# Twenty stores move from the SyncE queue to GpSimd, and sixteen gate loads are issued one product sooner

## The chip, the cores and the metric

The kernel runs on one core of one Trainium2 chip, as one launch. The core has TensorE (PE: matmuls, with a sequencer that loads weights, PEld), VectorE (DVE), ScalarE (ACT), GpSimd (POOL) and SyncE (SP). Each takes its own instructions in order and waits on semaphores for the others. DMA transfers are issued by SP, ACT and POOL and move data between on-chip memory and DRAM. The metric is device time in microseconds, the median of several executions.

## The reference

One decoder layer on x of shape 1 x 1024 x 1024, float32, cut to what matters here:

```python
h = rmsnorm(x, pre_g)
proj = h @ w_in    # [z_ssm | xBC | dt | q | k | v | f | z_att | g_ssm | g_att]
# A: Mamba-2 scan, 16 heads in 4 groups, 8 chunks of 128 positions
yg = ssd(conv_silu(xBC), dt) * silu(z_ssm)
y_ssm = yg * rsqrt(mean(yg*yg over the group) + eps) * ssm_norm_g
# B: forgetting attention, 16 heads, causal, softmax(q.k/8 + F[t] - F[s]) @ v
y_att = o * silu(z_att)
merged = sigmoid(g_ssm) * (y_ssm @ w_branch_ssm) + sigmoid(g_att) * (y_att @ w_branch_att)
out = x + rmsnorm(merged @ w_out, post_g)
```

The pieces that the change touches are y_ssm of the fourth group (the normed recurrence), silu(z_att) (attention's gates) and sigmoid(g_ssm) (the gates of the recurrence branch).

## The kernel before

**Products.** Every large matmul runs as three matmuls on high and low parts of the operands (names ending in h and l). The projection, the two branch products and the output product go through `Pair`: two blocks of 128 output columns times 1024 positions, done as seven products in the order 1, 2, 6, 5, 7, 4, 3 with sums of weights and of activations in place of an eighth. Each product is 12 matmuls of 128x512 into a PSUM bank (`pb`, `pc`, `pd`). Weights come by `raw<-in_wu` (L344, SP's queue, six buffers; a load waits for the last reader of the buffer that it overwrites), are summed on DVE (`sum`, L357 and L373; in place at L381), and split on ACT (L351) and DVE (L352) into `wop`, which has four buffers. `Pair.give` takes a finished product out of PSUM: ACT at L412, DVE at L414, L416 and L418. `keep` (L404) holds a partial one in `s`.

**Stages.** `Stream` is one fixed list of steps (pair, product) run in halves between other work. Until about 690 us that other work is the scan, group by group, with 8 chunks each. On POOL a chunk has `xe` (L872), `ce` (L879) and the state `new` (L893), which TensorE reads in its `yps` matmuls. At the end of a group `gate_and_norm` scales the four half rows `xs` (L1006) and stores them to `ys_dram` (L1010, SP's queue). Then comes attention, eight head pairs in six groups each: scores `s<-k,q`, a mask `far<-beyond` (`beyond` on POOL L1307, cast on DVE L1311), a row minimum on DVE (L1474, `nm`), the exponential on ACT (L1478, `ex`), transposes on TensorE (`pt`), copies `p` (L1515, L1517) and `av<-p,v`. The rest of the products runs between these groups.

**The pairs that matter.** The late pairs `za` (attention's silu gates, four pairs) run at the end of the scan and the start of attention. Their handler `silu_gate` does a tanh on ACT (L636), a multiply on DVE (L637) and the store `za_dram<-th` on SP's queue (L638). The pairs `gs` and `ga` store the tanh of the merge gates to `gs_dram` and `ga_dram` (ACT's queue, L622). From about 970 us the recurrence branch's product runs in four pairs with the handler `gated`: `begin` loads one 128x512 half of a gate (L1053, `th<-gs_dram`, SP's queue) as the step that finishes that half begins, and one half step after the result was taken from PSUM `times` multiplies it (L1062, DVE) and stores it from POOL (L1063, `ms_dram`). All of these 128x512 tiles named `th` come from one ring of four buffers (`small()`). In these pairs activations are fetched into `x0l` and the like on SP (L265) and split on ACT (L280, `x0h`) and DVE (L281). The mask rows `fb` are loaded on SP (L1335) and completed on POOL (L1342).

**What sets the order.** The program is written by a scheduler that places each instruction by its own estimate of when it can run, except for those pinned to program order; TensorE's order is fixed. Each engine then keeps its list. A DMA also waits for the one issued eight places before it in the same kind of queue, since eight semaphores go round for SP and ACT and eight for POOL. The instruction numbers in names (`th_6674`) are buffer numbers of the built program.

Of the kernel before, what the change touches and what calls it, by code (L numbers as in the profile page):

```python
# [23 lines left out]
NG = 4  # L24
# [62 lines left out]
def hybrid_layer(ctx: ExitStack, tc, a, out):  # L87

    nc = tc.nc
# [25 lines left out]
    za_dram = tc.dram_tile([NK, P, T], F32, name="za_dram")  # L115
    gs_dram = tc.dram_tile([NK, P, T], F32, name="gs_dram")
# [6 lines left out]
    ys_dram = tc.dram_tile([NK, P, T], F32, name="ys_dram")  # L123
# [8 lines left out]
    def turn(out_, in_, idn=ident):  # L132
        return tc.keep_in_program_order(nc.tensor.transpose(out_, in_, idn))  # L133

    def pin(op):
        return tc.keep_in_program_order(op)

    def small(name="th"):
        return gp.tile([P, HALF], F32, tag="th", name=name)
# [182 lines left out]
    class Pair:  # L322
# [95 lines left out]
                    nc.vector.tensor_tensor(d, s, ps, ALU.subtract)  # L418
            post(ch)

        def do(self, which):
            if which in (2, 4, 3) or which in (5, 7) and self.sums:
                unit, ch = {2: (0, 0), 4: (1, 0), 3: (0, 1)}.get(which, (1, 1))
                for begin in self.handlers[unit][2:]:
                    begin(ch)
            if which == 1:
                pool, tag = self.bank
                self.b = pool.tile([P, HALF], F32, tag=tag, bufs=1, name="pb")
                yield from self.matmuls(self.b, 1, "b11", True)
                self.k1 = self.keep(self.b)  # L430
            elif which == 2:
                pool, tag = self.other
                ps = pool.tile([P, HALF], F32, tag=tag, bufs=1, name="p" + tag)
                yield from self.matmuls(ps, 2, "b21", True)
                self.give(0, 0, ps, self.k1, "sum")
            elif which == 6:
                yield from self.matmuls(self.b, 6, "-t2", False)
                self.k2 = self.keep(self.b)
            elif which in (5, 7):
                if which == 5:  # L440
                    self.c = pj.tile([P, HALF], F32, tag="c", bufs=1, name="pc")
                    yield from self.matmuls(self.c, 5, "t1", True)
                else:
                    yield from self.matmuls(self.b, 7, "t3", False)
                    self.k7 = self.keep(self.b)
                self.sums += 1
                if self.sums == 2:
                    self.give(1, 1, self.c, self.k7, "less")
            elif which == 4:
                yield from self.matmuls(self.b, 4, "t4", False)  # L450
                self.give(1, 0, self.b)
            elif which == 3:
                yield from self.matmuls(self.c, 3, "-b22", False)
                self.give(0, 1, self.c, self.k2, "from")

    class Stream:
# [73 lines left out]
        def half(self):  # L530
            if self.run is None:
                if self.at == len(self.steps):
                    return False
                p, which = self.steps[self.at]
                if which == 7 and p.ops is ops_a and "merged" not in fin:
                    return False
                if p.ops is ops_a and not all(p.ops.ready(OPERAND[which].strip("-"), j) for j in range(KH)):
                    return False
                self.ahead(False)
                for ops in self.building:  # L540
                    ops.some(OPERAND[which])
                self.run = p.do(which)
                next(self.run)
            else:
                for _ in self.run:
                    pass
                self.run = None
                p, which = self.steps[self.at]
                if p in self.following:
                    ops = self.following[p]  # L550
                    if ops not in self.building:
                        self.building.append(ops)
                    ops.open(OPERAND[which])
# [12 lines left out]
            self.count += 1  # L566
            for w in self.waiting:
                w[0] -= 1
            for w in [w for w in self.waiting if w[0] <= 0]:
                self.waiting.remove(w)  # L570
                w[1]()
            return True
# [50 lines left out]

        return dst, post

    def silu_gate(dram, i):

        t = {}

        def dst(ch):  # L630
            t[ch] = small()
            return t[ch]

        def post(ch):
            th = small()
            nc.scalar.activation(th, t[ch], AF.Tanh, scale=0.5)  # L636
            nc.vector.scalar_tensor_tensor(th, th, 1.0, t[ch], ALU.add, ALU.mult)  # L637
            nc.sync.dma_start(dram[i, :, half(ch)], th)  # L638

        return dst, post  # L640

# [335 lines left out]
    def gate_and_norm(g):  # L977
        xs = [groups[g][f"xs{j}"] for j in range(2)]

        def flat(tag, bufs, name):  # L980
            return sp.tile([P, 4, P], F32, tag=tag, bufs=bufs, name=name).rearrange("p a b -> p (a b)")

        yield from squares(
            g, 1, [flat("csb", 2, "z") for _ in range(2)], [flat("m4", 2, "sqp").bitcast(F32R) for _ in range(2)],
            flat("ce", 1, "line")[0:1],
        )
        rc = groups[g]["rc"]
        nc.scalar.activation(rc, rc, AF.Sqrt, bias=eps4, scale=1.0 / 256.0)
        nc.vector.reciprocal(rc, rc)
        yield 3  # L990

        pr = pp.tile([P, HALF], F32, tag="tr", bufs=2, name="pr")
        turn(pr[0:NT, 0:P], rc)
        row = sp.tile([P, 4, P], F32, tag="ce", bufs=1, name="row")[0:NT, 0, :]
        nc.scalar.activation(row, pr[0:NT, 0:P], AF.Copy)
        nc.sync.dma_start(rr_dram[g].rearrange("(b p) -> b p", p=P), row)
        r = [sp.tile([P, 4, P], F32, tag="csb", bufs=2, name="r").rearrange("p a b -> p (a b)") for _ in range(2)]
        for ch in range(2):
            nc.sync.dma_start(r[ch], rr_dram[g : g + 1, half(ch)].to_broadcast([P, HALF]))
        yield 5  # L1000
        for ch in range(2):
            sl = half(ch)
            for j in range(2):
                i = 2 * g + j
                tc.keep_in_program_order(
                    nc.vector.scalar_tensor_tensor(  # L1006
                        xs[j][:, sl], xs[j][:, sl], ng[:, i : i + 1], r[ch], ALU.mult, ALU.mult
                    )
                )
                nc.sync.dma_start(ys_dram[i, :, sl], xs[j][:, sl])  # L1010
                yield 1

    def weights_work():
# [9 lines left out]
    def both(kind, i, handler):  # L1023
        return Pair(((kind, 2 * i), (kind, 2 * i + 1)), (handler(2 * i), handler(2 * i + 1)))
# [12 lines left out]
    order = [p for ps in by_group for p in ps]  # L1037

    order[0:4] = [both("gs", 0, lambda i: tanh_gate(gs_dram, i))] + [order[n] for n in (2, 1, 3, 0)]
    late = [both("za", g, lambda i: silu_gate(za_dram, i)) for g in range(4)]  # L1040
    late += [both("gs", g, lambda i: tanh_gate(gs_dram, i)) for g in range(1, 4)]
    late += [both("ga", g, lambda i: tanh_gate(ga_dram, i)) for g in range(4)]

# [2 lines left out]

    def gated(i):

        t = {}

        def begin(ch):
            t[ch] = small(), small()
            nc.sync.dma_start(t[ch][1], gs_dram[i, :, half(ch)])  # L1053

        def dst(ch):
            return t[ch][0]

        def post(ch):
            stream.after(1, lambda: times(*t[ch], ch))

        def times(y, g, ch):
            nc.vector.scalar_tensor_tensor(y, g, 1.0, y, ALU.add, ALU.mult)  # L1062
            pin(nc.gpsimd.dma_start(ms_dram[i, :, half(ch)], y))  # L1063

        return dst, post, begin
# [69 lines left out]
    with tc.tile_pool(name="pro", bufs=1, reuse_waits="tile", side="right") as pro, tc.tile_pool(  # L1135
# [12 lines left out]
        early = ExitStack()  # L1148
# [40 lines left out]
        stream = Stream(order + late + ends, len(order) + 3, len(order) + len(late) + 4)  # L1189
# [105 lines left out]
    with tc.tile_pool(name="att", bufs=1, reuse_waits="tile", side="right") as ap, tc.tile_pool(  # L1295
# [358 lines left out]
        for m in range(6 * NK + 1):  # L1654

            if m < 6 * NK:
                hp, g = divmod(m, 6)
# [104 lines left out]
```

## Time and profile before

| | us |
|---|---|
| runs | 1282.12, 1282.40, 1283.06 (median 1282.4) |
| profiled execution | 1286.04, of it span 1284.3 |
| TensorE busy | 1248.8 (97% of the span) |
| VectorE, ScalarE, GpSimd busy | 1015.3, 793.6, 311.5 |
| mean granted TensorE clock | 0.997 |

Busy times count compute instructions; DMA issues are not in them. The profile gives, for each instruction, its start, its duration and in brackets the idle time just before it with the instruction that ended it; PEld rows are weight loads, which lie beside matmuls. SPq, ACTq and POOLq are DMA issues on those engines' queues. Since TensorE is busy 97% of the span, the remaining idle spots on TensorE are where the span can shrink without work being removed. TensorE is idle for 35.5 us of the span. The first 60 us hold 16.2 of it, far from the change; what lies behind 640 us is mostly single waits of 0.2 to 2.3 us, and a tail in which the last rows are normed and stored.

### The profile page before, as it was taken

What the parts mean: (1) busy time and instruction counts of PE and PEld (TensorE: products, weight loads), DVE (VectorE), ACT (ScalarE), POOL (GpSimd) and SP (SyncE); (2) the same over time, 40 slices, a digit from 0 to 9 for tenths busy, and PEclk for the clock granted to TensorE, in tenths of its full rate; (3) what the DMA queues carried; (4) which work ended last, traced back from release to release, by engine and by line L of the source; (5) the groups of instructions that cost most, each with busy time, mean ns of one, the idle gap of its engine ahead of it and who ended that gap; (6) DMA issues with size and microseconds to landing.
All of it is one profiled execution on the core that took longest, in us unless ns stands there. A gap on an engine that the chain in (4) does not pass through costs nothing.

```text
span 1284.3 us, 20839 instructions
## 1 busy us (share of the span) xinstructions
PE 1248.8 (97%) x6926; PEld 982.4 (76%) x6926; DVE 1015.3 (79%) x1994; ACT 793.6 (62%) x1738; POOL 311.5 (24%) x314
## 2 busy tenths in 40 slices
PE   5999999999999999999999999999999999999997
PEld 3688878787888888888877777777767777778886
DVE  7988886987888978997767677767789766886976
ACT  7745665556664765566546666666677666753754
POOL 4000440013300241114102123322111212356052
PEclk9999999999999999999999999999999999999999
DMA  8232552646436543654356566675787657765932
GB/s 298 70 116 77 152 157 86 193 148 181 133 110 205 178 134 100 221 162 134 132 170 232 173 221 202 211 233 201 238 293 243 205 180 237 248 227 195 365 112 101
DMA packets 153516, 233.57 MB, mean 182 GB/s; under 512 B 15968, under 2 KB 61504, under 8 KB 153408
## 3 DMA queue, kind: packets, MB, share of 16 engines
q1 hardware_dynamic: 137408, 197.14, 48.0%
q10 hardware_dynamic: 11136, 19.11, 3.9%
q0 software_dynamic: 4864, 15.99, 3.2%
q8 instruction: 54, 0.88, 0.3%
q14 instruction: 54, 0.44, 0.1%
HBM read 162.99 MB, written 72.34 MB: 183 GB/s over the span
## 4 chain that ended last, share of the span: by engine, by line
PE 67%; DVE 11%; DMA 9%; issue 6%; ACT 5%; POOL 1%; SPq 1%; ACTq 0%; DVEq 0%; POOLq 0%
PE pb L130 29%; PE pc L130 16%; PE pd L130 6%; PE av L130 4%; PE pt L133 4%; PE s L130 3%; DVE wop L352 2%; PE yps L130 2%; DMA raw<-in_wu 1%; ACT ex L1478 1%; DVE sum L357 1%; DMA xt<-in_x 1%; ACT wop L351 1%; DMA rb<-st_dram 1%; PE tr_v L133 1%
## 5 line engine op out<-in xcount | busy, mean ns | idle before, releaser
L352 DVE TENSOR_TENSOR wop<-sum,wop 128x512 fp32r<-128x512 f32 x180 | 140.9, 784 | 53.6 <-ACT wop L351 52.4
L351 ACT ACTIVATE wop<-sum 128x512 fp32r<-128x512 f32 x180 | 112.4, 626 | 109.4 <-DVE sum L357 52.8
L1478 ACT ACTIVATE ex<-ex,nm 128x512 f32<-128x512 f32 (+1 forms) x192 | 116.2, 606 | 76.4 <-DVE nm L1474 74.4
L404 ACT ACTIVATE s<-pb 128x512 f32<-128x512 f32 x144 | 85.1, 591 | 92.1 <-PE pb L130 88.9
L130 PE MATMUL pc<-x3h,wop 128*128 128x512 f32 x384 | 129.8, 396 | 2.7 <-DVE th L414 2.3
L130 PE MATMUL pc<-x2h,wop 128*128 128x512 f32 x384 | 131.3, 400 | 1.0 <-DVE u L416 1.0
L130 PE MATMUL pb<-x0h,wop 128*128 128x512 f32 x384 | 130.8, 397 | 0.0
L130 PE MATMUL pb<-x6h,wop 128*128 128x512 f32 x384 | 129.5, 395 | 1.3 <-ACT s L404 1.3
L130 PE MATMUL pb<-x5h,wop 128*128 128x512 f32 x384 | 130.1, 396 | 0.7 <-ACT s L404 0.7
L130 PE MATMUL pb<-x4h,wop 128*128 128x512 f32 x384 | 129.2, 395 | 0.0
L352 DVE TENSOR_TENSOR wop<-raw,wop 128x512 fp32r<-128x512 f32 x144 | 106.2, 739 | 26.8 <-ACT wop L351 26.5
L1474 DVE CUSTOM_DVE_ANT_0 ex<-s,fb 128x512 f32<-128x512 f32 (+1 forms) x192 | 97.1, 552 | 20.9 <-PE s L130 15.2
L351 ACT ACTIVATE wop<-raw 128x512 fp32r<-128x512 f32 x144 | 89.6, 623 | 12.3 <-PE pd L130 5.9
L130 PE MATMUL pd<-x1h,wop 128*128 128x512 f32 x288 | 96.3, 394 | 0.0
L130 PEld LDWEIGHTS pc<-x3h,wop 128*128 128x128 f32 x384 | 72.1, 188 | 19.9 <-DVE th L414 2.7
L130 PEld LDWEIGHTS pc<-x2h,wop 128*128 128x128 f32 x384 | 72.6, 189 | 18.8 <-issue 2.4
L130 PEld LDWEIGHTS pb<-x6h,wop 128*128 128x128 f32 x384 | 72.1, 188 | 18.6 <-issue 2.0
L130 PEld LDWEIGHTS pb<-x5h,wop 128*128 128x128 f32 x384 | 72.1, 188 | 18.5 <-issue 2.0
L130 PEld LDWEIGHTS pb<-x0h,wop 128*128 128x128 f32 x384 | 72.1, 188 | 17.4 <-issue 2.9
L130 PEld LDWEIGHTS pb<-x4h,wop 128*128 128x128 f32 x384 | 72.1, 188 | 16.8 <-issue 1.9
L213 POOL TENSOR_TENSOR wd<-wd 128x256 f32<-128x256 f32 x32 | 33.7, 1052 | 206.3 <-DMA wd<-in_wo 119.7
L133 PE MATMUL pt<-ident,ex 128*128 128x128 f32 x576 | 76.7, 276 | 4.4 <-DVE nm L1474 2.4
(311 smaller groups left out, 2986.4 us busy)
## 6 DMA issues: line engine op xcount, KB each, us to landing
raw<-in_wu SPq DMA_DIRECT2D x128, 256.0 KB
csb<-cs_dram SPq DMA_DIRECT2D x32, 256.0 KB
fb<-f_dram SPq DMA_DIRECT2D x16, 512.0 KB
rb<-st_dram SPq DMA_DIRECT2D x48, 128.0 KB
wd<-in_wo SPq DMA_DIRECT2D x40, 128.0 KB
xt<-in_x SPq DMA_DIRECT2D x8, 512.0 KB
gs_dram<-th ACTq DMA_DIRECT2D x16, 256.0 KB
qh_dram<-th ACTq DMA_DIRECT2D x16, 256.0 KB
```

The costliest lines, as they stand in the source:

```text
L130: return tc.keep_in_program_order(nc.tensor.matmul(*args, **kw))
L133: return tc.keep_in_program_order(nc.tensor.transpose(out_, in_, idn))
L213: pin(nc.gpsimd.tensor_tensor(t[out_], t[a_], t[b_], ALU.subtract))
L351: nc.scalar.activation(op[:, 0], src, AF.Copy)
L352: nc.vector.tensor_tensor(op[:, 1], src, op[:, 0], ALU.subtract)
L357: self.adds.tensor_tensor(t, x, y, ALU.add)
L404: nc.scalar.activation(s, ps, AF.Copy)
L1474: nc.vector.tensor_tensor_reduce(o, s[e][:, 0:w], fb[hp, h][:, e, 0:w], 1.0, 3.0e38, ALU.add, ALU.min, nm)
L1478: pin(nc.scalar.activation(o, o, AF.Exp, scale=-1.0, bias=nm, accum_out=hd.at(hd.sm, i, h, e)))
```

## The change

First, the four `ys_dram` stores of the last group and all sixteen `za_dram` stores are issued by POOL instead of SP. Second, the gate load of `gated.begin` is marked early: `Stream.half` calls it as it starts the step ahead of the one that needs it, so the load is written one product sooner, and the result's tile is taken only at `dst`.

```diff
+        def begin(self, which, sums, early):
+            if which in (2, 4, 3) or which in (5, 7) and sums:
...
+                    if hasattr(begin, "early") == early:
+                        begin(ch)
...
+                if self.at + 1 < len(self.steps):
+                    after, then = self.steps[self.at + 1]
+                    after.begin(then, after.sums + (after is p and which in (5, 7)), True)
                 self.run = p.do(which)
...
-    def silu_gate(dram, i):
+    def silu_gate(dram, i, queue=nc.sync):
...
-            nc.sync.dma_start(dram[i, :, half(ch)], th)
+            queue.dma_start(dram[i, :, half(ch)], th)
...
-                nc.sync.dma_start(ys_dram[i, :, sl], xs[j][:, sl])
+                queue = nc.sync if g < NG - 1 else nc.gpsimd
+                queue.dma_start(ys_dram[i, :, sl], xs[j][:, sl])
...
-    late = [both("za", g, lambda i: silu_gate(za_dram, i)) for g in range(4)]
+    late = [both("za", g, lambda i: silu_gate(za_dram, i, nc.gpsimd)) for g in range(4)]
...
         def begin(ch):
-            t[ch] = small(), small()
-            nc.sync.dma_start(t[ch][1], gs_dram[i, :, half(ch)])
+            g[ch] = small()
+            nc.sync.dma_start(g[ch], gs_dram[i, :, half(ch)])
+
+        begin.early = True
```

TensorE's list is the same in both kernels. Three places of the others follow; line numbers of the changed kernel are 7 to 11 higher.

SP's list where the scan ends and attention begins (`raw` are weight loads, `r` the norm's factors, `q` and `k` attention's operands), before:

```order
L344 DMA raw_6584<-in_wu 128x512
L344 DMA raw_6586<-in_wu 128x512
L1010 DMA ys_dram_92<-xs0_5373 128x512
L1010 DMA ys_dram_92<-xs1_5482 128x512 x2
L638 DMA za_dram_84<-th_6624 128x512
L1010 DMA ys_dram_92<-xs0_5373 128x512
L1326 DMA q_6724<-qh_dram_87 128x256
L1326 DMA q_6724<-ql_dram_88 128x256
L1333 DMA k_6727<-kh_dram_89 128x512
L638 DMA za_dram_84<-th_6674 128x512
L344 DMA raw_6682<-in_wu 128x512
L344 DMA raw_6684<-in_wu 128x512
```

The same place after:

```order
L344 DMA raw_6584<-in_wu 128x512
L344 DMA raw_6586<-in_wu 128x512
L344 DMA raw_6682<-in_wu 128x512
L344 DMA raw_6684<-in_wu 128x512
L1337 DMA q_6724<-qh_dram_87 128x256
L1337 DMA q_6724<-ql_dram_88 128x256
L1344 DMA k_6727<-kh_dram_89 128x512
L1344 DMA k_6727<-kl_dram_90 128x512
```

The six stores that stood between the two pairs of weight loads are gone from SP, and the loads of q and k stand behind the second pair (`raw_6682`, `raw_6684`) instead of ahead of it.

POOL's list at the last chunks of the last group, before:

```order
L893 TENSOR_TENSOR new_6150<-new_6046,cdec_641 128x256
L872 TENSOR_TENSOR xe_6163<-xdt_6141,tend_640 128x256
L879 TENSOR_TENSOR ce_6165<-ce_6165,ct_5119 128x512
L893 TENSOR_TENSOR new_6245<-new_6150,cdec_641 128x256
L879 TENSOR_TENSOR ce_6256<-ce_6256,ct_5119 128x512
L213 TENSOR_TENSOR wd_1264<-wd_1264,wd_1265 128x256
L1307 AFFINE_SELECT beyond_6715<-big_6714 128x192 x2
L1342 TENSOR_TENSOR fb_6730<-fb_6730,far_6712 64x2x128 x4
```

The same place after, with stores between:

```order
L645 DMA za_dram_84<-th_6100 128x512
L213 TENSOR_TENSOR wd_1265<-wd_1264,wd_1265 128x256
L900 TENSOR_TENSOR new_6150<-new_6046,cdec_641 128x256
L879 TENSOR_TENSOR xe_6163<-xdt_6141,tend_640 128x256
L886 TENSOR_TENSOR ce_6165<-ce_6165,ct_5119 128x512
L645 DMA za_dram_84<-th_6225 128x512
L900 TENSOR_TENSOR new_6245<-new_6150,cdec_641 128x256
L886 TENSOR_TENSOR ce_6256<-ce_6256,ct_5119 128x512
L645 DMA za_dram_84<-th_6300 128x512
L645 DMA za_dram_84<-th_6338 128x512
L213 TENSOR_TENSOR wd_1264<-wd_1264,wd_1265 128x256
L645 DMA za_dram_84<-th_6367 128x512
```

A store now stands ahead of the state and the operand of the last chunk (`new_6245`, `ce_6256`), and another ahead of the chunk before. Behind these rows eleven more `za` and `ys` stores stand ahead of `beyond_6715`.

DVE's list late in attention, around the third recurrence pair's multiply by a gate (`th_11672` before, `th_11615` after; the `ISA` rows are the row minimum), before:

```order
L352 TENSOR_TENSOR wop_11668<-raw_11001,wop_11668 128x512
L1062 TENSOR_SCALAR th_11671<-th_11672,th_11671 128x512
L1474 ISA ex_6723,nm_11565<-s_11692,fb_11536 128x512
L1474 ISA nm_11565 128x1
L352 TENSOR_TENSOR wop_11734<-raw_10999,wop_11734 128x512
L1474 ISA ex_6723,nm_11565<-s_11693,fb_11536 128x512
L1474 ISA nm_11565 128x1
L281 TENSOR_TENSOR x0l_11631<-x0l_11631,x0h_11630 128x512 x2
L1474 ISA ex_6723,nm_11565<-s_11704,fb_11536 128x512
L1474 ISA nm_11565 128x1
L1474 ISA ex_6723,nm_11565<-s_11705,fb_11536 128x512
```

The same place after:

```order
L352 TENSOR_TENSOR wop_11670<-raw_11001,wop_11670 128x512
L352 TENSOR_TENSOR wop_11736<-raw_10999,wop_11736 128x512
L281 TENSOR_TENSOR x0l_11633<-x0l_11633,x0h_11632 128x512 x2
L1073 TENSOR_SCALAR th_11687<-th_11615,th_11687 128x512
L1485 ISA ex_6723,nm_11565<-s_11694,fb_11535 128x512
L1485 ISA nm_11565 128x1
L1485 ISA ex_6723,nm_11565<-s_11695,fb_11535 128x512
L1485 ISA nm_11565 128x1
L1485 ISA ex_6723,nm_11565<-s_11706,fb_11535 128x512
L1485 ISA nm_11565 128x1
L1485 ISA ex_6723,nm_11565<-s_11707,fb_11535 128x512
```

The multiply now stands behind a split of weights and the splits of `x0l`, and the four row minima follow it without anything between. On SP the load of this gate stands ahead of the `x0l` loads (behind them before).

More of the change, by code (lines that the diff above doesn't have):

```diff
@@ L419, in give, with do @@
             post(ch)
-        def do(self, which):
-            if which in (2, 4, 3) or which in (5, 7) and self.sums:
+        def begin(self, which, sums, early):
+            if which in (2, 4, 3) or which in (5, 7) and sums:
                 unit, ch = {2: (0, 0), 4: (1, 0), 3: (0, 1)}.get(which, (1, 1))
                 for begin in self.handlers[unit][2:]:
-                    begin(ch)
+                    if hasattr(begin, "early") == early:
+                        begin(ch)
+        def do(self, which):
+            self.begin(which, self.sums, False)
             if which == 1:
@@ L1047, in gated @@
     def gated(i):
-        t = {}
+        y, g = {}, {}
         def begin(ch):
-            t[ch] = small(), small()
-            nc.sync.dma_start(t[ch][1], gs_dram[i, :, half(ch)])
+            g[ch] = small()
+            nc.sync.dma_start(g[ch], gs_dram[i, :, half(ch)])
+        begin.early = True
         def dst(ch):
-            return t[ch][0]
+            y[ch] = small()
+            return y[ch]
         def post(ch):
-            stream.after(1, lambda: times(*t[ch], ch))
+            stream.after(1, lambda: times(y[ch], g[ch], ch))
         def times(y, g, ch):
```

## The prediction

> **What bounds the kernel now.** First the page's table of busy shares:
>
> ```profile
> span 1284.3 us, 20839 instructions
> PE 1248.8 (97%) x6926; PEld 982.4 (76%) x6926; DVE 1015.3 (79%) x1994; ACT 793.6 (62%) x1738; POOL 311.5 (24%) x314
> ```
>
> TensorE sets the time. Its list does not change, so the change can only move TensorE's idle spots. The next view is TensorE's timeline behind 640 us; in brackets stands the idle time ahead of a row and what ended it. These are its spots near the places that the change reorders:
>
> ```profile
> 676.37 0.50 PE L130 MATMUL pc<-x3h,wop 128*128 128x512 f32 x1 [2.32 <-DVE th L414]
> 1083.58 0.33 PE L133 MATMUL pt<-ident,ex 128*128 128x128 f32 x1 [1.30 <-DVE nm L1474]
> 1084.19 1.93 PE L133 MATMUL pt<-ident,ex 128*128 128x128 f32 x13 [0.28 <-DVE nm L1474]
> ```
>
> Together they are 2.32 + 1.30 + 0.28 = 3.90 us. The chain of waits says what stands behind each (start, duration, what):
>
> ```profile
> 667.66 0.42 SPq L344
> 668.18 6.72 DMA raw<-in_wu
> 675.02 0.06 DVE sum L357
> 675.63 0.69 DVE th L414
> ...
> 1063.20 0.70 DVE o L1438
> 1072.66 6.41 DMA th<-gs_dram
> 1079.20 0.06 DVE th L1062
> ```
>
> At 676 us TensorE waits for a PSUM bank that DVE empties (L414). DVE stands in its list at a sum of two weight blocks that are still in flight. At 1084 us it waits for row minima, which stand in DVE's list behind the multiply by a gate (L1062), whose load came late. Both causes are transfers issued on SP's queue.
>
> **Part 1, stores from SP to POOL.** SP's timeline between the weight loads:
>
> ```profile
> 652.45 0.91 SPq L344 DMA_DIRECT2D raw<-in_wu  x2
> ...
> 658.90 5.50 SPq L1010 DMA_DIRECT2D ys_dram<-xs  x3
> 664.69 0.32 SPq L638 DMA_DIRECT2D za_dram<-th  x1
> 665.35 0.32 SPq L1010 DMA_DIRECT2D ys_dram<-xs  x1
> ...
> 667.23 0.38 SPq L638 DMA_DIRECT2D za_dram<-th  x1
> 667.66 0.94 SPq L344 DMA_DIRECT2D raw<-in_wu  x2
> ```
>
> From 658.90 to 667.6 us SP goes through six stores, each of which waits for a DVE result; q and k loads fill the gaps left out. Only then come the two loads. Without the stores they wait for the last readers of their buffers alone. DVE's rows give these, the landing and what follows:
>
> ```profile
> 656.28 0.69 DVE L357 TENSOR_TENSOR sum<-raw 128x512 f32<-128x512 f32 x1 [2.80 <-DMA raw<-in_wu]
> 660.78 0.69 DVE L381 TENSOR_TENSOR raw<-raw 128x512 f32<-128x512 f32 x1
> 665.24 1.29 DVE L352 TENSOR_TENSOR wop<-raw,wop 128x512 fp32r<-128x512 f32 x2
> 668.93 0.66 DVE L637 SCALAR_TENSOR_TENSOR th<-th 128x512 f32<-128x512 f32 x1
> 670.05 0.66 DVE L1311 CAST far<-beyond 64x192 bf16<-64x192 f32 x2 [0.45 <-POOL beyond L1307]
> 675.02 0.69 DVE L357 TENSOR_TENSOR sum<-raw 128x512 f32<-128x512 f32 x1 [3.59 <-DMA raw<-in_wu]
> ```
>
> The first buffer is free at 660.78 + 0.69 = 661.5, the second after the first of the two splits of 665.24, at 665.9. So the later load goes at 666.0 instead of 668.2. Its landing is bounded by two pairs. The pair of 652.45, its second load about 0.46 later, was in use at 656.28, at most 3.4 us from issue; the pair of 667.66 took 6.72. The sum may then start between 669.4 and 672.7. I take the early end, since the q and k loads that were ahead now stand behind the pair.
>
> DVE's list now goes: multiply of 668.93 (to 669.6), sum, split, casts of `far`, eviction L414. The casts need `beyond` from POOL, and POOL now stands at the store of that multiply's result. One issue on POOL is measured below at 0.55 us, and a POOL store started 0.3 us after its producer there. So the store ends at 669.6 + 0.3 + 0.55 = 670.45, `beyond` (two, 0.64 us) at 671.1, the casts at 671.8, L414 at 672.5. TensorE is ready at 676.37 − 2.32 = 674.05. The whole 2.32 us go, with 1.5 us to spare. With the late landing the sum ends at 673.4, the split and casts at 674.7, L414 at 675.4 instead of 676.3: 0.9 of the 2.32 us go. Late next are the mask rows, and they have until the first scores, 10 us later.
>
> What POOL pays: 20 issues, 11 us, on an engine busy 24%. These rows price them (a group, the line's view, two of POOL's timeline, DVE's, TensorE's):
>
> ```profile
> L1548 POOL DMA_DIRECT2D ya_dram<-zr x14 | 7.7, 551 | 109.2 <-DVE zr L1432 55.1 <-DVE zr L1439 54.1
> DMA to landing us min/median/max: 2.3/4.4/5.3
> 1080.18 0.54 POOL L1063 DMA_DIRECT2D ms_dram<-th  x1 [6.43 <-DVE th L1062]
> 617.36 1.78 POOL L879 TENSOR_TENSOR ce<-ce,ct 128x512 f32<-128x512 f32 x1 [3.31 <-ACT ce L878]
> 617.91 1.78 DVE L637 SCALAR_TENSOR_TENSOR th<-th 128x512 f32<-128x512 f32 x1
> 622.74 0.39 PE L130 MATMUL yps<-ce,new 128*64 128x128 f32 x4
> ```
>
> The row of 1080.18 gives the 0.3: its multiply ran from 1079.20 for 0.69. POOL's order decides at one spot. Ahead of the last chunk's `new` and `ce` stands a store that waits for the multiply of 617.91, done at 619.7. In DVE's list that multiply now stands ahead of the chunk's state update, so it should end about a microsecond sooner. By the old time the store ends at 620.5, `new` (0.61) at 621.1, `ce` (1.78 in its slowest form) at 622.9, against 622.74 for its matmul: 0.2 us. With the earlier multiply there is a microsecond to spare. I take 0, range 0 to +0.2. The group's other stores follow one another with the multiplies, and TensorE has no matmul behind POOL there until `beyond`. The landing counts too: L414 writes a ring tile whose store is the one SP issued at 667.23. From POOL it goes at about 667.5; with 0.55 and the 4.4 us median it is down at 672.4 at the latest, ahead of 673.4, where L414 has to start. At the 5.3 us maximum it is 673.3, still just in time.
>
> The Trainium skill ("DMA: Bandwidth & Descriptors", section "Issuing engines are not separate DMA queues") speaks against this part: transfers started by different engines run on the same 16 DMA engines and interleave, so another issuer saves only sequencer time. By that rule the bytes around 667 us still share the engines, the landing stays at 6.72 us, the part is worth 0.9 us, and the sum would be 1279.9. No row of this trace shows the loads without stores beside them, so it stays among the rivals.
>
> **Part 2, gate loads a product sooner.** Sixteen loads, none added. Two of them ended a DVE wait before; the multiply of 1048.94 cost TensorE nothing, this one did:
>
> ```profile
> 1072.66 0.38 SPq L1053 DMA_DIRECT2D th<-gs_dram  x1
> 1076.92 1.14 ACT L280 ACTIVATE x0h<-x0l 128x512 fp32r<-128x512 f32 x2
> 1079.20 0.69 DVE L1062 SCALAR_TENSOR_TENSOR th<-th 128x512 f32<-128x512 f32 x1 [5.55 <-DMA th<-gs_dram]
> 1081.63 1.29 DVE L281 TENSOR_TENSOR x0l<-x0l,x0h 128x512 fp32r<-128x512 f32 x2
> 1083.44 0.69 DVE L1474 CUSTOM_DVE_ANT_0 ex<-s,fb 128x512 f32<-128x512 f32 x1
> ```
>
> After, the load stands ahead of the `x0l` loads and waits only for its ring tile, which the multiply of 1063.20 frees at 1063.9. Issued at 1064.5, even at 6.41 us it lands by 1071. DVE then waits for ACT instead: a split of weights, the `x0h` pair, and the eviction that the scheduler put behind them, about 1075.9 + 0.5 + 1.1 + 0.6 = 1078.2. DVE does its split, the `x0l` pair (1078.5), the multiply (1079.1) and four row minima at 0.6 each: the third ends at 80.95, the fourth at 81.55 (before: 1083.52, 1084.13). TensorE ran its first two transposes at 1081.90, so both waits of 1.30 and 0.28 go: 1.58 us. Bounds: nothing if ACT comes 2 us later, 1.58 if as worked out. I take 1.58. The price is on SP: early loads can wait for ring tiles with `rb`, q and k loads queued behind them, by 0.8 to 2 us on the stores' landings; the loads behind have more time than that before use. 0, with +1 as the far end.
>
> **The sum.** 1286.04 (1284.3 of span and 1.7 around it) − 2.32 − 1.58 = 1282.1. The profiled execution stands 3.6 us above the median of 1282.4, so for the runs: 1282.4 − 3.9 = 1278.5.
>
> **The rivals.** 0.2% of 1282.4 is 2.6 us, about what a measurement of this kernel can tell from no change.
>
> One stall stays: a landing as late as before keeps 1.4 of the 2.32 (1279.9), a POOL backlog over 1.5 us ahead of `beyond` all of it (1282.4 − 1.58 = 1280.8), or ACT 2 us late keeps the 1.58 (1280.1). All are within 0.2%. For it speaks that two of these limits are only 1.5 to 2 us away.
>
> Nothing gained: the order settles so that another late load takes both places; DVE's ring of four tiles ties each multiply to a store's landing. 1282.4.
>
> More than the sum. The profile has one stretch at half clock, behind a 1.61 us wait:
>
> ```profile
> 957.67 0.44 PE L133 MATMUL pt<-ident,ex 128*128 128x128 f32 x2 [1.61 <-ACT ex L1478]
> 940.00:960.00 20.00, 17.07 (x112) 12.43 (x111) 15.44 (x38) 13.31 (x34) 1.81 (x3) 0.96 0.80 274
> 960.00:980.00 20.00, 19.89 (x123) 14.75 (x122) 17.57 (x45) 16.32 (x43) 3.49 (x5) 0.87 0.79 272
> ```
>
> In the 20 us windows the granted clock is 0.96 and 0.87: (0.04 + 0.13) × 20 = 3.4 us. A shift of a microsecond may spare it: 1275.1. Against: its wait comes from ACT, which the change hardly touches.
>
> Slower: POOL waits in order. The longest wait of SP for such a multiply is in this row of the waits of its queue:
>
> ```profile
> SPq L638 <- DVE th L637: 82.8, 22, 8.3
> ```
>
> If POOL inherits 8.3 us ahead of the last `ce`, which had 622.74 − 619.14 = 3.6 us to spare, TensorE idles 4.7 us, and a second half-clock stretch like that above follows (3.4): 1278.5 + 8.1 = 1286.6. It decides once POOL is held over 3.6 us there. Against it: the multiply is due 0.6 us after the old `ce`.
>
> The Trainium skill ("DMA: Bandwidth & Descriptors", section "SWDGE vs HWDGE vs iDMA") has GpSimd write descriptors into on-chip memory that DVE locks it out of in one of its modes. That would lengthen issues beside a full DVE; the 14 issues above at 551 ns mean show none of it.
>
> **How the numbers follow.** Both stalls go, 0.54; more than that, 0.08; one stays, 0.15; nothing, 0.10; slower, 0.13. Faster: 0.54 + 0.08 = 0.62, same 0.25, slower 0.13. The likeliest gives 1278.5, with a range of its own from 1277.5 (an estimated 1 us of small waits behind a full DVE that may shrink) to 1279.7 (0.2 at `ce`, 1 on SP). The range for 8 in 10 reaches down to the half-clock case, 1275.0, and up over no gain to 1285.0, short of most of the slower case.
>
> **What would show it.** Step by step: SP issues the two `raw` loads by 666.5 back to back; DVE's sum starts by 670; no wait over 0.3 us ahead of `pc<-x3h,wop` near 674; POOL issues each store in 0.55 us; `yps<-ce,new` of the last chunk without a wait; no wait for `th<-gs_dram`; the transposes near 1080 in one row. It is wrong if a new wait on TensorE over 1 us appears between 600 and 700 us or behind an `rb` or mask load in attention, or if a second half-clock stretch shows.

## The result, and the profile after

| | before | after |
|---|---|---|
| median of 22 runs each, us | 1283.79 | 1280.99 |
| lowest and highest, us | 1281.15, 1285.89 | 1279.38, 1286.31 |
| profiled execution, us | 1286.04 | 1283.55 |

The ratio is 0.9982, 95% interval 0.9975 to 0.9988: 0.18% of 1283.8 are 2.3 us less, between 1.5 and 3.2 (the two medians by themselves lie 2.8 apart). A gain of 3.9 had been forecast, so some 1.6 of it are missing. Set on the 1282.4 from which the forecast started, the ratio gives 1280.1, above the 1277.5 to 1279.7 that went with the likeliest case.

The page after, first lines:

```profile
span 1281.9 us, 20857 instructions
PE 1249.7 (97%) x6926; PEld 984.5 (77%) x6926; DVE 1015.8 (79%) x1994; ACT 795.3 (62%) x1738; POOL 321.7 (25%) x334
```

POOL has its twenty instructions more, TensorE is as busy as before. POOL's busy time grows by 10.2 us, so the busy time of POOL does hold its DMA issues, other than the section on the time before says. The two waits are gone, as the steps said. This is DVE's timeline after, at the first place:

```profile
651.60 0.69 DVE L357 TENSOR_TENSOR sum<-raw 128x512 f32<-128x512 f32 x1 [1.36 <-DMA raw<-in_wu]
652.21 0.68 DVE L414 TENSOR_TENSOR th<-pd,s 128x512 f32<-128x512 f32 x1
...
668.07 0.69 DVE L357 TENSOR_TENSOR sum<-raw 128x512 f32<-128x512 f32 x1 [0.17 <-DVE th L644]
669.87 0.53 DVE L1322 CAST far<-beyond 64x192 bf16<-64x192 f32 x2
670.83 0.69 DVE L414 TENSOR_TENSOR th<-pc,s 128x512 f32<-128x512 f32 x1 [0.42 <-PE pc L130]
```

The sum of 668.07 no longer waits for its loads, and L414 of 670.83 now waits for TensorE instead of the reverse. (In the second and third profile of after it waits 0.6 us for a store from POOL; TensorE is not ready in these either.) The later load of the pair is issued at 664.01 and has landed 3.98 us later, where it took 6.72 in the first profile of before. POOL's timeline shows its part, each issue 0.54 to 0.58 us here:

```profile
617.37 0.58 POOL L645 DMA_DIRECT2D za_dram<-th  x1 [4.85 <-DVE th L644]
617.97 0.62 POOL L900 TENSOR_TENSOR new<-new,cdec 128x256 f32<-128x256 f32 x1
618.54 1.30 POOL L886 TENSOR_TENSOR ce<-ce,ct 128x512 f32<-128x512 f32 x1
...
668.20 0.54 POOL L645 DMA_DIRECT2D za_dram<-th  x1 [2.17 <-DVE th L644]
668.74 0.65 POOL L1318 TENSOR_SCALAR_AFFINE_SELECT beyond<-big 128x192 f32<-128x192 f32 x2
```

The last chunk's `ce` is done at 619.84, ahead of its matmul at 621.56 us. At the second place the transposes run in one row, and these rows of TensorE's timeline after are what is new:

```profile
654.15 0.50 PE L130 MATMUL pb<-x5h,wop 128*128 128x512 f32 x1 [0.42 <-ACT s L404]
1078.37 1.91 PE L133 MATMUL pt<-ident,ex 128*128 128x128 f32 x16
1112.29 1.28 PE L130 MATMUL s<-k,q 64*128 64x256 f32 x7 [1.33 <-ACT p L1528]
1122.14 0.50 PE L130 MATMUL pc<-x3l,wop 128*128 128x512 f32 x1 [0.49 <-DVE x3l L281]
```

The wait at 654.15 comes from the sum of 651.60 above: DVE stands at it for its load, L414 behind it is late, and ACT, which waits for L414 with a tanh, is late with the eviction L404. ACT's row of that tanh, before and after:

```profile
652.11 0.63 ACT L636 ACTIVATE th<-th 128x512 f32<-128x512 f32 x1 [0.74 <-DVE th L414]
```

```profile
652.98 0.63 ACT L643 ACTIVATE th<-th 128x512 f32<-128x512 f32 x1 [2.86 <-DVE th L414]
```

Behind 1112.29 the windows (busy times by engine, then granted clock, DMA share, GB/s) show a stretch of lower clock; (1 − 0.72) × 5 are 1.4 us, and 0.3 in the window ahead:

```profile
1110.00:1115.00 5.00, 3.42 (x25) 2.20 (x25) 2.49 (x4) 5.00 (x12) 2.80 (x3) 0.94 0.48 163
1115.00:1120.00 5.00, 5.00 (x26) 3.32 (x23) 4.63 (x15) 2.68 (x11) 0.69 (x2) 0.72 0.35 104
```

So something is given back at two places: near 654, and between 1100 and 1145 us.

### The profile page after: what moved, and what is told of

It reads as the page before. It is cut to its first block, busy times and chain, and to the rows that moved or that the text cites. A ratio compares the mean times of both kernels' runs of the same rounds, so it can differ in the third digit from the quotient of the medians.

```text
span 1281.9 us, 20857 instructions
## 1 busy us (share of the span) xinstructions
PE 1249.7 (97%) x6926; PEld 984.5 (77%) x6926; DVE 1015.8 (79%) x1994; ACT 795.3 (62%) x1738; POOL 321.7 (25%) x334
## 4 chain that ended last, share of the span: by engine, by line
PE 75%; DVE 9%; DMA 7%; ACT 5%; issue 3%; SPq 1%; DVEq 0%; ACTq 0%
PE pb L130 31%; PE pc L130 18%; PE pd L130 5%; PE av L130 5%; PE pt L133 5%; PE s L130 5%; PE yps L130 2%; DVE wop L352 2%; DMA raw<-in_wu 1%; DVE sum L357 1%; DMA xt<-in_x 1%; PE st L130 1%; PE tr L133 1%; ACT wop L351 1%; DMA ql_dram<-th 1%
## 5 line engine op out<-in xcount | busy, mean ns | idle before, releaser
L404 ACT ACTIVATE s<-pb 128x512 f32<-128x512 f32 x144 | 85.2, 592 | 99.7 <-PE pb L130 98.0
```

The lines of the kernel that those rows point to most:

```text
L404: nc.scalar.activation(s, ps, AF.Copy)
```

## The experiments

TensorE's list of 6926 matmuls is the same in every kernel here. So each matmul of one profile can be set beside the same matmul of another, and the table says how much longer (+) or shorter (−), in us, a stretch between two matmuls took than in the first profile of before. Stretches are named by that profile's times. "Unchanged" adds 230 to 640 and 700 to 1060 us. Rows change place there only from 603 and from 968 us on, and behind these two times the fourteen profiles agree within 0.2 us; so what this column shows is scatter. The other four columns hold the rest of the changed rows and what they lead to. A break costs a little more than its bracket says, since matmuls that follow without one overlap: the 1.30 us near 1084 us delay the next matmuls by 1.46.

| profile | unchanged | 640–662 | 662–700 | 1060–1100 | 1100–1145 |
|---|---|---|---|---|---|
| before, first | 0 | 0 | 0 | 0 | 0 |
| before, second | +0.4 | 0.00 | −0.87 | −0.34 | +0.60 |
| before, third | −0.8 | 0.00 | −0.87 | −0.83 | −0.33 |
| gates alone | −2.5 | 0.00 | −0.74 | −2.33 | +1.26 |
| stores alone | −1.2 | +0.59 | −2.37 | +0.03 | +2.05 |
| after, first | −1.9 | +0.71 | −2.36 | −2.33 | +3.49 |
| after, second | +1.0 | +0.73 | −2.37 | −2.03 | 0.00 |
| after, third | −0.3 | +0.33 | −2.37 | −2.33 | −0.15 |
| all but the 14th gate | −2.9 | +0.37 | −2.39 | −1.93 | +1.63 |
| 11th gate only | +1.2 | +0.58 | −2.37 | −2.33 | +1.17 |
| all but the 15th gate | −2.5 | +0.54 | −2.37 | −2.33 | +1.57 |
| first twelve gates, first | −1.5 | +0.25 | −2.28 | −2.21 | +0.16 |
| first twelve gates, second | −2.4 | +0.59 | −2.37 | −2.32 | +1.07 |
| late stores, twelve gates | −0.1 | 0.00 | −0.67 | −2.25 | +0.53 |

The first column differs by −2.9 to +1.2 us between executions, as much as the whole effect; the three profiles of after alone, one and the same program, lie 2.9 apart. Single times therefore say little here, and the stretches say more.

### Each part alone

The first theory (A) blamed the load of the fourteenth gate half. In the first profile of after, DVE waited 2.08 us for rb near 1101 us, and this gate load stands ahead of the rb loads on SP.

Stores alone takes the early mark away:

```diff
-        begin.early = True
```

> Only the stores move to POOL; the gate loads stay as before. Theory A (the two waits go as forecast, and what is given back comes from the fourteenth gate load, which stands ahead of the rb loads in SP's list and holds DVE at o<-o,rb near 1101 us): the 2.32 us wait near 674 us is gone, the 1.58 us near 1084 us stay, no wait over 0.5 us near 1112 us; with 0.4 us new near 654 us some 1.9 us faster than before, ratio near 0.9985. Theory B (stores from POOL load the DMA engines so that a ya_dram store and rb land late): TensorE waits about 1.3 us near 1112 us here too, ratio near 1.000. Theory C (most of the difference between the two profiles is scatter between executions, since 1.6 us of it stand ahead of the first changed row): ratio within 0.1% of 1 whatever the waits.

Measured: ratio 0.9996, 0.9985 to 1.0006. The 2.32 us near 674 us are gone. The second place keeps its waits, and a wait near 1112 us is there without any early gate. That is what theory B had said, and theory A had not. TensorE's rows of this kernel:

```profile
1080.82 0.33 PE L133 MATMUL pt<-ident,ex 128*128 128x128 f32 x1 [1.33 <-DVE nm L1483]
1081.43 1.92 PE L133 MATMUL pt<-ident,ex 128*128 128x128 f32 x13 [0.28 <-DVE nm L1483]
1114.57 1.28 PE L130 MATMUL s<-k,q 64*128 64x256 f32 x7 [1.27 <-ACT p L1526]
1126.29 0.87 PE L130 MATMUL av<-p,v 128*64 128x256 f32 x8 [0.96 <-ACT p L1526]
```

Gates alone leaves the stores on SP:

```diff
-    late = [both("za", g, lambda i: silu_gate(za_dram, i, nc.gpsimd)) for g in range(4)]
+    late = [both("za", g, lambda i: silu_gate(za_dram, i)) for g in range(4)]
...
-                queue = nc.sync if g < NG - 1 else nc.gpsimd
+                queue = nc.sync
```

> Only the gate loads are early; the stores stay on SP. Theory A: the 2.32 us near 674 us stay, the 1.58 us near 1084 us go, and a wait of some 1.3 us near 1112 us with a stretch of lower clock behind it gives back about 3.5: 1 to 2 us slower than before, ratio near 1.001. Theory B: no wait near 1112 us, 1.6 us faster, ratio near 0.9988. Theory C: ratio within 0.1% of 1.

Measured: ratio 0.9993, 0.9978 to 1.0007. Three rows of it, TensorE's, DVE's and TensorE's again:

```profile
675.10 0.50 PE L130 MATMUL pc<-x3h,wop 128*128 128x512 f32 x1 [0.76 <-DVE th L414]
...
1113.29 0.69 DVE L418 TENSOR_TENSOR th<-s,pc 128x512 f32<-128x512 f32 x1 [1.91 <-DMA st_dram<-st]
...
1120.27 0.50 PE L130 MATMUL pc<-x3l,wop 128*128 128x512 f32 x1 [1.47 <-DVE x3l L281]
```

The wait that the stores were to remove is 0.76 us here, with SP's stores where they were. Near 1112 us TensorE waits 0.48, not 1.3. And a third thing shows: DVE stands at L418 for the store of an 8x128 strip (`st`), and TensorE waits for the operand splits queued behind it on DVE. Neither interval is clear of 1: theory C, a ratio within 0.1% of 1 in both, is the one whose sign came out, and of A's signs for this kernel only one did, that the 1.58 us near 1084 us go.

### Which gate

The next kernels select single halves:

```diff
-                    if hasattr(begin, "early") == early:
+                    if (ch in getattr(begin, "early", ())) == early:
...
-        begin.early = True
+        begin.early = (0,) if i == 7 else (0, 1)
```

That is all but the fourteenth; only the eleventh is `(0,) if i == 5 else ()`.

> Both parts, but the load of one half of a gate (the fourteenth of sixteen) is not early: in all lists one row of SP's differs from the changed kernel, this load, which stands behind the rb loads again. Theory A: DVE's wait at o<-o,rb falls from 2.08 to about 1.3 us or less, TensorE's near 1112 us from 1.33 to under 0.7, without a stretch of lower clock; 1.5 to 3 us faster than the changed kernel, ratio to before near 0.9965. Theory B: wait and time as in the changed kernel, ratio near 0.998.

> Stores on POOL, and of the gate loads only the eleventh, whose lateness ended the wait near 1084 us, is early. Theory A: both forecast waits go (2.32 and 1.58 us), nothing over 0.5 us near 1112 us: 3 to 4 us faster than before, ratio near 0.997. Theory B: a wait of about 1.3 us near 1112 us as in the changed kernel, ratio near 0.998.

Measured: 0.9984 for both (0.9976 to 0.9993, and 0.9971 to 0.9997). Without the fourteenth, DVE's wait for rb is 0.18 us and TensorE's near 1112 us 0.68: the row moved does what A says of it. That may be scatter, since in the second and third profile of after, whose row stands as in the first, DVE does not wait for rb at all. And L418 waits 2.51 us for the strip and TensorE 1.65 behind it, so the stretch still takes +1.63, and stores alone has the wait near 1112 us without that load. Theory A falls as the cause of the give-back. With the eleventh alone, both waits are gone: one load of sixteen makes the second gain. It is 2.1 us faster than before, where A had 3 to 4. Its wait near 1112 us is 0.35 us, so 1.3 us there does not come with stores on POOL either, as B had it. In twelve of the fourteen profiles TensorE's wait at this place is DVE's wait for rb near 1101 us within 0.03 us (1.27 and 1.26 in stores alone, 0.88 and 0.86 without the fifteenth gate, 0.48 and 0.46 in gates alone).

The strip explains itself in the built program. All `th`, `st` and `rb` tiles share the ring of four, and an earlier gate load shifts which tile each later result gets. The last L418 of the pair waits, before and after:

```
before: L418 th_12130<-s_11821,pc_11990  waits for POOL DMA 0, DVE, PE
after:  L418 th_12182<-s_11823,pc_11989  waits for POOL DMA 4, DVE, HW DMA 2, PE, ACT
```

HW DMA 2 is the strip's store. In each of the five profiles with this tile, L418 starts 0.12 or 0.13 us after that store has landed. Leaving the fifteenth half late (`(1,) if i == 7 else (0, 1)`) gives this result another tile; so does leaving the last four late (`(0, 1) if i < 6 else ()`).

> The changed kernel, but the load of the fifteenth gate half is not early, so that the last L418 of the pair does not take the tile of the 8x128 strip but one that a DVE instruction frees. If that ring tile causes the give-back behind 1112 us: no wait over 0.5 us of DVE at L418 near 1114 us, TensorE's wait near 1121 us under 0.4 us, about 1 us faster than the changed kernel. If it does not: TensorE's wait near 1121 us is 0.5 to 1.7 us as in the other runs with all gates early.

> The changed kernel with the first twelve gate halves early and the last four as before: neither a gate load ahead of the rb loads nor the strip's tile under L418. If these two are what the change gives back: no wait over 0.5 us of TensorE between 1100 and 1130 us except the 0.69 us for s<-pb that every run has, ratio to before near 0.997 (both forecast waits gone, 0.3 to 0.5 us lost near 654 us). If the give-back is the DMA engines' bandwidth instead, 1 to 2 us of waits stay between 1100 and 1130 us and the ratio is near 0.998.

Measured: 0.9981 (0.9969 to 0.9993) and 0.9968 (0.9951 to 0.9985). DVE no longer stands at L418 and TensorE does not wait for `x3l` in either. In all five profiles that have the strip's tile, that wait is 0.49 to 1.65 us (mean 0.99); in the nine others it is at most 0.36 (mean 0.10). So the ring tile costs 0.9 us at that place, and this is shown. It does not make the stretch longer than it is without the tile, though: from 1100 to 1145 us the five take 1.2 us more than the first profile of before, and the six with stores on POOL and another tile 1.1. Something else comes in its place: without the fifteenth TensorE waits 0.88 us near 1110 and 0.95 at `av<-p,v` near 1122 us, and with twelve gates 0.45 at the latter, a row where before has no wait. Stores alone has this wait too (0.96). It stands behind an ACT eviction whose ring tile is still being stored. ACT's timelines of stores alone and of before, each with the row of that eviction:

```profile
1123.60 0.60 ACT L412 ACTIVATE th<-pb 128x512 f32<-128x512 f32 x1 [1.97 <-DMA ms_dram<-th]
```

```profile
1124.35 0.60 ACT L412 ACTIVATE th<-pb 128x512 f32<-128x512 f32 x1 [1.07 <-DMA ms_dram<-th]
```

ACT waits for the same kind of store in both. In the three profiles of before it waits 0.72 to 1.07 us and TensorE has no wait behind it; in the six profiles with stores on POOL and without the strip's tile it waits 1.46 to 2.04 us, and TensorE 0.39 to 0.96 (mean 0.65). The eviction starts 4.2 to 4.5 us after POOL's issue of that store in before, and 4.9 to 5.5 in the six. So the store that POOL already had lets go some 0.9 us later there. None of the kernels changes that store, its issuer or its size. The traces show something beside it. Such a store reports its landing in sixteen parts, and in the six profiles the fifteenth is in after 4.1 to 4.8 us and the last alone comes 0.3 to 0.9 us behind it; in before the last follows within 0.2. In all six an 8 KB packet of the queue that the profile calls instruction starts 2.8 to 3.5 us after the issue, while the store is under way; in before it starts after 4.7 to 5.0, when the store has landed. Over the stores from POOL into `za_dram`, `ys_dram`, `ya_dram` and `ms_dram` in the fourteen profiles whose fifteenth part came 3 to 5 us after the issue, the last part trails it by 0.47 us (median of 73) with such a packet on the way and by 0.16 (of 210) without. That fits a packet of instructions that holds up one part of the store, but no run moves it by itself, so the cause is not shown.

### The same kernels again

> The kernel before, unchanged, profiled a second time, for the scatter of its waits. If the waits that the forecast priced are properties of the program, TensorE's 2.32 us near 676 us (behind the sum of two weight loads) and 1.30 + 0.28 us near 1084 us come again within 0.3 us. If a wait for a transfer differs from one execution to the next, the one near 676 us lies anywhere from 0.5 to 2.5 us, since the same lists gave 0.76 us in the run with the stores still on SP; the 1.58 us near 1084 us should repeat even then, since DVE's list and not only the landing makes it.

> The kernel before a third time, for the scatter. If the 2.32 us near 676 us were the upper end of a wait that scatters, TensorE waits 0.5 to 2 us there this time; the waits near 1084 us are 1.0 to 1.6 us again.

> The changed kernel, profiled a second time. Waits that its lists make come again: no wait near 676 and 1084 us, 0.3 to 0.5 us near 654 us, DVE's wait of 1.9 to 2.5 us at L418 near 1114 us (its result takes the ring tile of an 8x128 strip whose store is still under way), and 0.5 to 1.7 us of TensorE behind it near 1121 us. If the wait of 1.33 us near 1112 us and the stretch of lower clock behind it were scatter, they are smaller this time, under 0.8 us and with a clock of 1.00.

> The changed kernel a third time, with rounds. If the waits between 1100 and 1145 us scatter with the landing of transfers, this stretch takes between 0 and 3.5 us more than in the first profile of before; the stretches of the two forecast waits repeat (640 to 700 us within 0.4 us of 1.65 less, 1060 to 1100 us within 0.4 us of 2.2 less). Ratio to before 0.9975 to 0.9990.

Before, second profile: TensorE's timeline, then the load in the chain of waits:

```profile
676.13 0.50 PE L130 MATMUL pc<-x3h,wop 128*128 128x512 f32 x1 [0.90 <-DVE th L414]
```

```profile
669.36 5.30 DMA raw<-in_wu
```

The third profile, in the same order:

```profile
675.08 0.50 PE L130 MATMUL pc<-x3h,wop 128*128 128x512 f32 x1 [1.05 <-DVE th L414]
```

```profile
668.06 5.55 DMA raw<-in_wu
```

The load that took 6.72 us in the first profile takes 5.30 and 5.55 here, and TensorE waits 0.90 and 1.05 instead of 2.32. Of the sixteen parts of the 6.72, fifteen had landed after 4.73: one late part makes the difference. In the second profile 0.36 stand a little earlier in the same stretch. At the second place the pairs of waits are 0.96 + 0.28 and 0.49 + 0.28 instead of 1.30 + 0.28. Of four profiles with the stores on SP the first is the worst at the first place, and of the four with late gates the second worst at the second.

After, second and third: the stretches of the two waits repeat, and the one from 1100 to 1145 us takes 0.00 and −0.15. The wait of 1.33 us near 1112 us and the lower clock behind it do not come again; the strip's tile does, with 0.69 and 0.64 us of TensorE at `x3l`. DVE's wait at L418 is 0.75 and 0.71 us instead of the 1.9 to 2.5 that were expected: the strip's store landed 1.2 us after its issue here and took 2.4 to 3.0 in the other three. The runs beside the third profile gave a ratio of 0.9998, 0.9985 to 1.0011, outside the 0.9975 to 0.9990 that were expected, against 0.9982 for the 22 runs of the result. The effect is small enough that two sets of executions of the same pair differ by it.

### The early sum near 654 us

```diff
-    late = [both("za", g, lambda i: silu_gate(za_dram, i, nc.gpsimd)) for g in range(4)]
+    late = [both("za", g, lambda i: silu_gate(za_dram, i, nc.gpsimd if i >= 4 else nc.sync)) for g in range(4)]
```

This keeps the first eight `za` stores on SP, with the first twelve gates early. The scheduler then leaves the sum behind L414 near 651 us, as before.

> Of the attention gates' stores only those of the last two pairs, with the four of the normed recurrence, are on POOL; the first eight stay on SP. The first twelve gate halves are early. DVE's list near 651 us is that of before again (the sum of two weight loads behind the eviction L414, not ahead of it), while the weight loads near 665 us stay ahead of q and k. If the order of that sum costs the 0.3 to 0.5 us: TensorE does not wait near 654 us and still not near 674 us, and the stretch from 640 to 662 us takes within 0.1 us of before instead of 0.25 to 0.73 more. If the new wait comes from POOL's stores or the transfers: 0.2 us or more stay. Ratio to before near 0.997, 0.3 to 0.5 us under the twelve-gate kernel, which the rounds alone may not resolve.

> The kernel with the first twelve gate halves early and all twenty stores on POOL, a second time, beside the changed kernel on the same chip. If its give-back between 1100 and 1145 us (0.16 us in its first profile, against 0.00 to 3.49 with all sixteen early) comes from the list, it stays under 0.6 us and the time is 1 to 2 us under the changed kernel's, ratio to before near 0.997. If it was a lucky execution: 1 us or more of give-back and a ratio near 0.998.

Measured: 0.9979 (0.9965 to 0.9993) for the late stores, 0.9980 (0.9969 to 0.9991) for the twelve gates a second time. The stretch 640–662 is 0.00 with the late stores, and +0.25 to +0.73 in all nine profiles whose list has the sum ahead: the order of that sum costs it. (This kernel also has the first eight stores back on SP; the rows of DVE and ACT near 652 us, shown with the result, are what puts it down to the sum.) But 662–700 gives −0.67 only. Rows of the late stores, POOL's, DVE's, TensorE's:

```profile
668.22 0.54 POOL L645 DMA_DIRECT2D za_dram<-th  x1 [1.27 <-DVE th L644]
...
670.44 0.69 DVE L357 TENSOR_TENSOR sum<-raw 128x512 f32<-128x512 f32 x1
...
674.44 0.69 DVE L414 TENSOR_TENSOR th<-pc,s 128x512 f32<-128x512 f32 x1 [1.66 <-PE pb L130]
...
675.19 0.50 PE L130 MATMUL pc<-x3h,wop 128*128 128x512 f32 x1 [0.80 <-DVE th L414]
```

The sum is on time, and L414 is late all the same. In the program it also waits for the store of the tile that it overwrites, the one issued at 668.22; that store's last completion in the trace is at 674.35, 6.1 us after its issue, just ahead of 674.44. The profile names the PE product that ended near then. In the second profile of after the same wait is named as it is:

```profile
673.15 0.69 DVE L414 TENSOR_TENSOR th<-pc,s 128x512 f32<-128x512 f32 x1 [0.64 <-DMA za_dram<-th]
```

There TensorE was not yet ready, and it cost nothing. The twelve gates with all twenty stores on POOL gave 0.9968 and 0.9980 in two sets, the second beside after's 0.9998 on the same chip. The stretch 1100–1145 takes +1.07 the second time, after +0.16 the first: by the sign given ahead of it (1 us or more), the first was a lucky execution. The intervals of 0.9980 and 0.9998 overlap, so that this kernel beats the change is not shown.

## Why the prediction was right or wrong

**In short.** Both waits went by the mechanism that was forecast, and over three profiles each the two stretches gave 3.6 us of the 3.9. The step that failed is the price: the sum took 0 for part 1 (at most +0.2) and 0 for part 2 (at most +1), where the profiles show 0.6 near 654 us and 1.0 between 1100 and 1145 us. The rival "one stall stays" (1279.9 to 1280.8) comes nearer by its number and is wrong by its mechanism, since neither stall stays.

**The mechanism of part 1: right.** The loads go as soon as their buffers are free, the sum starts at 668.07, which is 668.6 on the clock of before (the profile of after is 0.6 us ahead there) against 669.4 as put, and L414 is done before TensorE needs it. The rival of a landing as late as before did not come: the later load took 3.98 us in the first profile of after and 3.58 and 4.09 in the others. POOL's 0.55 us, the multiply that ends sooner, `ce` in time: all as put. The two loads are not issued back to back, as the signs had it, but at 659.56 and 664.01, each within 0.03 us of the last reader of its own buffer. No issue beside a full DVE took over 0.76 us.

**The size of part 1: wrong, the step "the whole 2.32 us go".** The number is that of one execution, in which the later load took 6.72 us. Over the three profiles of before the stretch 662–700 is 0.58 us shorter than in the first, and over those of after 2.37. What was there to gain was 2.37 − 0.58 = 1.8. The text noted that this execution stood 3.6 us above the median and carried the whole wait over to the median all the same.

**A cost taken at nothing: wrong, the list near 651 us.** The prediction looked at the sum of 668 us alone. The same move put another sum ahead of an eviction 17 us earlier, where its load is not in yet (1.36 us of DVE in the row above). That is 0.59 us of TensorE over the three profiles of after. The net of part 1 is 1.2 instead of 2.3.

**The term of part 2: right in its mechanism, and near in size by some luck.** 1060–1100 is 0.39 shorter over the profiles of before and 2.23 over those of after: 1.84 against a forecast 1.58. The waits priced at 1.58 are 1.58, 1.24 and 0.77 in the three profiles, 1.20 in the mean; that a break costs more than its bracket makes up for it.

**The price of part 2: wrong, "the price is on SP … 0, with +1 as the far end".** Order on SP was looked at, the ring and the scatter of landings were not. The prediction's own signs of being wrong came in the first profile of after: a wait of 1.33 us behind rb and a second stretch of lower clock. The last result of the pair gets the tile of a strip that is still being stored, 0.9 us of TensorE as measured at `x3l`. Where it gets another tile, the later release of the `ms` store takes 0.65 us in its place. Over the three profiles each, 1100–1145 gives back 1.11 − 0.09 = 1.0. This 1.0 is the mean of 3.49, 0.00 and −0.15, so it rests on one execution; and stores alone takes +2.05 there in its one profile and gates alone +1.26, so the runs do not say which part has to pay it.

**The sum of the measured terms:** −1.8 + 0.6 − 1.84 + 1.0 = −2.0 us, against −2.3 (−3.2 to −1.5) from the runs. That the two agree so well is luck in part, as the last term shows.

**The margin of the store under L414** was given as "at the 5.3 us maximum … still just in time". It took 6.1 us in one experiment and then was the wait. In the changed kernel it ended before TensorE was ready. **The slower rival** did not occur: POOL held nothing that TensorE waits for. **The half-clock stretch near 958 us** is in all three profiles of after, in two of them for 3.41 us instead of 6.83, a loss of 1.7 us instead of 3.4; it did not go in any.

**What stays open.** The stretch 1100–1145 us ranges from −0.33 to +3.49 over all profiles, and with late gates it also reaches +2.05. There the DMA engines are full (a share of 1.05 from 1100 to 1105 us in the first profile of after), and DVE's wait for rb was between 0 and 2.08 us. Whether early gates make that wait more frequent, these fourteen profiles do not tell. Nor do they show why the `ms` store lets go later in the six profiles named above; the instruction packet is a lead.

## What to carry to other kernels

A wait for a transfer in one profile is a draw, not a price: profile the kernel twice or three times before a wait of a microsecond or two goes into a sum at its full size. Small prices need the same care as the gains: here the gains came out at 3.6 of 3.9 us, and prices put at nothing took 1.6 of them. Where a change moves a tile's first or last use, list for the whole ring which earlier user each later tile now waits for, not only what moved. When a scheduler pulls one instruction forward, look for every other one that it pulled forward with it.

## What the runs showed of the hardware

The stretches of the table's first column took up to 2.9 us less and 1.2 us more than in the first profile of before, out of 1280, so that a sum over waits seen once cannot be better than that. The clock stretch near 958 us follows a pair of waits of 1.3 to 2.9 and 0.9 us in every profile. The granted clock is at half there for 3.41 us in eight of the profiles and for 6.83 in six, never in between, which costs 1.7 or 3.4 us; the longer wait does not go with the longer stretch. In the first profile of after it was at half for 3.41 us once more, behind a wait of 1.33 us near 1112 us, and in stores alone a wait of 1.27 us at the same place left it at 1.00. A 256 KB store of a gate from POOL took 2.3 us at the least and 7.1 at the most to land in the first profile of after, with a median of 3.0. Of the sixteen parts in which a transfer reports its landing, the last can come well behind the rest: 2.0 us in the load that made the wait of 2.32.
